# Three pairs of adaLN units through one PSUM bank each, one pair moved onto the second value unit

## The chip, the cores and the metric

The kernel runs on one core of one Trainium2 chip. The metric is the device time of one execution in microseconds, and of several runs the median. The core's engines are TensorE (PE in the profile, with its weight loads as PEld), VectorE (DVE), ScalarE (ACT), GpSimd (POOL) and SyncE (SP), whose queue issues nearly all of the DMAs.

## The reference, cut to what matters

One layer of a streaming encoder is computed for a prompt of 1024 rows and a sample of 32 rows. A conditioning vector for each of the two gives six vectors of 1024 numbers, which scale and shift the rows:

```
mod = jax.nn.silu(c) @ w_ada + b_ada
sh1, sc1, g1, sh2, sc2, g2 = jnp.split(mod[:, None, :], 6, axis=-1)
h = x * (1 + sc1) + sh1
...split(h @ w_in, split_at, axis=-1)        # keys, queries, values of three kinds of heads, gates
mix = jnp.concatenate([mLSTM heads, FoX heads, gated MLP], axis=-1) @ w_o
x = _layer_norm(ALPHA * x + (1 + g1) * mix, ln1_g, ln1_b)
h = x * (1 + sc2) + sh2
y = (jax.nn.silu(h @ w_gate) * (h @ w_up)) @ w_down
x = _layer_norm(ALPHA * x + (1 + g2) * y, ln2_g, ln2_b)
```

`w_ada` has 1024 rows and 6144 columns. `c` is one vector for the prompt and one for the sample, so its product has two rows.

## The kernel before, in words

**adaLN units.** The 6144 columns of `w_ada` are laid out as 24 units of 256 columns. Units 0 to 7 give sh1 and sc1, units 8 to 15 sh2 and sc2, units 16 to 19 g1, units 20 to 23 g2. `ada_load` loads a unit as two tiles of 128x1024 floats (512 KB each), one for each half of the 1024 rows. `ada_parts` then does the unit's work. Eight matmuls of 256 columns (two halves by four quarters of a half; each is two passes in the trace) use a weight tile of 32 columns, `c32`, in which columns 0 and 1 hold the two conditioning vectors and the others are zero. The quarter `k` of a half goes to the PSUM partitions from 32k on, so the two rows of the result stand four times, as partial sums. ACT copies the 128x256 block to `adas`, PE transposes it in two 128x128 pieces into the other half of the same bank (pool `pt`, two banks), and a reduction of DVE into `adam` adds the four partial sums. `ada_end` adds the bias and writes `mod`.

**Where the units stand.** Units 0 to 7 run inside `fm_first`, the first projection. In `run` the list `rest` holds units 16 to 19 and then 8 to 15, and `more(n)` does the next n of them with the tiles `late` (two buffers in pool `pl`). The tuple `T1` says how many come before the first value unit, between the two value units, after the second, and after the first step of the gates: 1, 1, 0, 2. The others come one by one among the heads (`a` in `ORDER`). Units 20 to 23 come near the end of the first half, among the last three key and query units (heads 5, 6, 7): 20 and 21 after head 5, 22 after head 6, 23 after head 7, with six buffers `late`.

**The value units.** `tm_unit` with `w_in_v` computes 264 columns (four heads of values and some gate columns) for nine tiles of rows: first the 32 sample rows (tile 8, 64 small matmuls from the raw weights `tm_raw`), then eight tiles of 128 rows, 24 matmuls each (`tm_g`, pool `pg`, three banks). Weights are split into a high part (ACT, `tm_whi`) and a low part (DVE, `tm_wlo`). `evac_v` copies each bank by ACT into `tm_traw` (two buffers), which the queue of SP stores to `o_v`; DVE makes `tm_vhl` (two buffers) of it, stored to `dv`.

**What sets the order.** `fm_first` is pinned in the order written. The rest is ordered by a scheduler that works on modelled times, so that a step can end up between the steps of another function; `tie` can hold instructions behind a given one. All engines run their instructions in that order. The DMAs of SP's queue are issued in the queue's order, and one that waits for its data or its buffer holds back those behind it.

## Time and profile before

| | |
|---|---|
| median of 3 runs | 1350.47 us (1349.51 to 1352.93) |
| the profiled execution | 1349.43 us, of it 1347.7 us span from the first to the last instruction |
| PE busy | 1326.7 us, 98% of the span |
| DVE, ACT, POOL busy | 992.0, 657.6, 229.2 us |
| mean granted PE clock | 0.997 |
| DMA | 221.73 MB, mean 165 GB/s |

In the profile's timeline a row gives the start in us, the duration, the engine, the line and operation, the tile written and the tiles read, the number of instructions merged into the row, and in brackets the idle time of the engine before it with what ended it. Matmuls are pipelined: the durations of neighbours overlap, so the time that a step takes on PE is read from one start to the next.

### The profile page before, as it was taken

What the parts mean: (1) busy time and instruction counts of PE and PEld (TensorE: products, weight loads), DVE (VectorE), ACT (ScalarE), POOL (GpSimd) and SP (SyncE); (2) the same over time, 40 slices, a digit from 0 to 9 for tenths busy, and PEclk for the clock granted to TensorE, in tenths of its full rate; (3) what the DMA queues carried; (4) which work ended last, traced back from release to release, by engine and by line L of the source; (5) the groups of instructions that cost most, each with busy time, mean ns of one, the idle gap of its engine ahead of it and who ended that gap; (6) DMA issues with size and microseconds to landing.
All of it is one profiled execution on the core that took longest, in us unless ns stands there. A gap on an engine that the chain in (4) does not pass through costs nothing.

```text
span 1347.7 us, 25627 instructions
## 1 busy us (share of the span) xinstructions
PE 1326.7 (98%) x9690; PEld 1209.8 (90%) x9690; DVE 992.0 (74%) x2094; ACT 657.6 (49%) x1308; POOL 229.2 (17%) x263
## 2 busy tenths in 40 slices
PE   9999999999999999999999999999999999999996
PEld 6789888988999888888888888999999999999995
DVE  5635665678779677686876766678988897888777
ACT  3423445454546544545455354436764453635355
POOL 0101100153246100000000000463710000000341
PEclk9999999999999999999999999999999999999998
DMA  9584566545667744454433433673695858554221
GB/s 363 208 288 152 159 193 195 174 118 193 178 225 232 215 123 137 118 146 121 141 107 111 127 87 98 205 186 114 183 266 141 224 152 222 137 177 133 87 79 67
DMA packets 119450, 221.73 MB, mean 165 GB/s; under 512 B 18580, under 2 KB 62768, under 8 KB 119328
## 3 DMA queue, kind: packets, MB, share of 16 engines
q1 hardware_dynamic: 112096, 207.55, 48.9%
q0 software_dynamic: 6032, 11.94, 5.2%
q8 instruction: 76, 1.25, 0.4%
q10 hardware_dynamic: 1200, 0.62, 0.2%
q14 instruction: 46, 0.38, 0.1%
HBM read 188.13 MB, written 51.85 MB: 178 GB/s over the span
## 4 chain that ended last, share of the span: by engine, by line
PE 71%; DVE 3%; ACT 1%; DMA 1%; issue 0%; DVEq 0%; ACTq 0%
PE up_g L129 6%; PE up_g L130 6%; PE up_g L131 6%; PE dn_g L129 4%; PE dn_g L131 4%; PE dn_g L130 4%; PE sup_u L129 3%; PE sup_u L131 3%; PE sup_u L130 3%; PE wo_g L129 2%; PE wo_g L131 2%; PE wo_g L130 2%; PE sup_g L131 2%; PE sup_g L130 2%; PE sup_g L129 2%; PE fox_t L936 2%
## 5 line engine op out<-in xcount | busy, mean ns | idle before, releaser
L130 PE MATMUL up_g<-tm_al,up_whi 128*128 128x512 f32 (+1 forms) x384 | 140.5, 366 | 0.0
L129 PE MATMUL up_g<-tm_ah,up_whi 128*128 128x512 f32 (+1 forms) x384 | 140.1, 365 | 0.0
L131 PE MATMUL up_g<-tm_ah,up_wlo 128*128 128x512 f32 (+1 forms) x384 | 139.4, 363 | 0.0
L1361 ACT CAST sup_whi<-sup_raw 128x1024 fp32r<-128x1024 f32 x54 | 56.0, 1047 | 90.6 <-PE dn_u L130 47.2
L129 PEld LDWEIGHTS up_g<-tm_ah,up_whi 128*128 128x128 f32 x384 | 72.2, 188 | 11.2 <-issue 0.4
L131 PEld LDWEIGHTS up_g<-tm_ah,up_wlo 128*128 128x128 f32 x384 | 72.3, 188 | 11.0
L130 PEld LDWEIGHTS up_g<-tm_al,up_whi 128*128 128x128 f32 x384 | 72.3, 188 | 10.9
L1192 DVE SCALAR_TENSOR_TENSOR wo_z<-dn_g,start_mod,wo_z 128x512 f32<-128x512 f32 (+4 forms) x120 | 60.3, 521 | 26.0 <-PE dn_g L131 25.2
L909 ACT ACTIVATE fox_p<-fox_s,fox_fmx 128x384 f32<-128x384 f32 (+2 forms) x96 | 55.1, 578 | 48.0 <-DVE fox_fmx L907 34.0
L116 ACT CAST up_whi<-up_raw 128x1024 fp32r<-128x1024 f32 x50 | 52.4, 1047 | 51.6 <-PE up_g L130 23.3
L1362 DVE TENSOR_TENSOR sup_wlo<-sup_raw,sup_whi 128x1024 fp32r<-128x1024 f32 x54 | 68.1, 1264 | 10.8 <-ACT sup_whi L1361 10.8
L117 DVE TENSOR_TENSOR up_wlo<-up_raw,up_whi 128x1024 fp32r<-128x1024 f32 x50 | 65.2, 1303 | 13.9 <-ACT up_whi L116 11.6
L131 PE MATMUL dn_g<-up_acth,dn_wlo 128*128 128x512 f32 (+2 forms) x200 | 73.4, 367 | 0.0
L129 PE MATMUL dn_g<-up_acth,dn_whi 128*128 128x512 f32 (+2 forms) x200 | 73.2, 367 | 0.0
L130 PE MATMUL dn_g<-up_actl,dn_whi 128*128 128x512 f32 (+2 forms) x200 | 72.8, 365 | 0.0
L941 ACT CAST fox_pth<-fox_t 128x512 fp32r<-128x512 f32 (+1 forms) x80 | 41.8, 542 | 62.5 <-PE fox_t L936 56.5
L116 ACT CAST dn_whi<-dn_raw 128x1024 fp32r<-128x1024 f32 (+1 forms) x44 | 42.7, 970 | 52.3 <-PE up_g L130 18.9
L904 DVE TENSOR_REDUCE fox_fmx<-fox_s 128x1 f32<-128x384 f32 (+2 forms) x96 | 52.8, 553 | 18.7 <-PE fox_s L901 17.6
L942 DVE TENSOR_TENSOR fox_ptl<-fox_t,fox_pth 128x512 fp32r<-128x512 f32 (+1 forms) x80 | 50.0, 632 | 12.5 <-ACT fox_pth L941 12.1
L397 PE MATMUL tm_g<-tm_whi,start_h1h 128*128 128x256 f32 (+1 forms) x192 | 55.3, 288 | 0.7 <-DVE tm_traw L470 0.7
L397 PE MATMUL tm_g<-tm_whi,start_ah 128*128 128x256 f32 (+1 forms) x192 | 54.8, 286 | 0.5 <-DVE tm_brt L457 0.5
L398 PE MATMUL tm_g<-tm_wlo,start_h1h 128*128 128x256 f32 (+1 forms) x192 | 55.1, 287 | 0.0
(682 smaller groups left out, 4762.7 us busy)
## 6 DMA issues: line engine op xcount, KB each, us to landing
up_raw<-w_gu SPq DMA_DIRECT2D x50, 512.0 KB
ada_late<-w_ada SPq DMA_DIRECT2D x32, 512.0 KB
dn_raw<-w_dn SPq DMA_DIRECT2D x28, 512.0 KB
sup_raw<-w_gu SPq DMA_DIRECT2D x20, 512.0 KB
start_dp<-w_gu SPq DMA_DIRECT2D x19, 512.0 KB
start_dp<-w_gu POOLq DMA_DIRECT2D x19, 512.0 KB, 7.8
wo_raw<-w_o SPq DMA_DIRECT2D x18, 512.0 KB
sup_raw<-start_dp SPq DMA_DIRECT2D x18, 512.0 KB
```

The source lines that it names most:

```text
L116: nc.scalar.copy(hi[:, :w], raw[:, :w])
L117: (eng or nc.vector).tensor_tensor(lo[:, :w], raw[:, :w], f(hi[:, :w]), ALU.subtract)
L129: nc.tensor.matmul(ps, hi, xh(k), start=start and k == 0, stop=False)
L130: nc.tensor.matmul(ps, hi, xl(k), start=False, stop=False)
L131: self.lastmm = nc.tensor.matmul(ps, lo, xh(k), start=False, stop=stop and k == n - 1)
L397: nc.tensor.matmul(ps[:, :ncol], xh, hi, start=k == 0, stop=False)
L398: nc.tensor.matmul(ps[:, :ncol], xh, lo, start=False, stop=False)
L904: nc.vector.tensor_reduce(mxs[:, x:x + 1], s[:, :w], AX.X, ALU.max, negate=True)
L909: nc.scalar.activation(pr[:, lo:hi], banks[x][:, :hi - lo], AF.Exp, bias=mxs[:, 0:1], accum_out=sums[:, x:x + 1])
L1192: self.lastz = self.nc.vector.scalar_tensor_tensor(z[:, m, x:y], ps[:, x - a:y - a], g[i], z[:, m, x:y], ALU.mult, ALU.add)
L1361: nc.scalar.copy(h, x)
L1362: tt(l, x, f(h), ALU.subtract)
```

## The change

`ada_parts` takes a list of units. With two of them it issues all 16 matmuls into one bank: the weights of the second are read from `c32` with an offset, so that its two rows come to stand behind those of the first, and `c32` is 38 columns wide for it, the two vectors in columns 6 and 7. There is then one copy, one pair of transposes and one reduction (into 2 by 8 columns) for both units; `ada_end` runs for each.

Units 16 and 17 form a pair. Its four tiles get a pool of their own, `pe`, with four buffers on the other side of the memory, and it is emitted behind tile 0 of the second value unit, its PE instructions held behind that tile's last matmul. `T1` becomes (0, 0, 0, 2). Units 20 and 21 form a pair after head 6, units 22 and 23 one after head 7; nothing stands after head 5 any more. All other units stay single. The tiles `ct` and `ce`, which are used only at the start, are taken from the weights' buffers in place of the constants' pool.

```diff
-T1 = (1, 1, 0, 2)
+EB = 4
+T1 = (0, 0, 0, 2)
...
-        self.ct = t([P, KT, 2], "ct")
+        self.ct = self.t(self.wp, [P, KT, 2], F32, "whi", WB)
...
-        e = t([P, KT, 2], "ce")
+        e = self.t(self.wp, [P, KT, 2], F32, "wlo", WB)
...
-    def ada_parts(self, u, raws, ppool, ptag):
+    def ada_parts(self, units, raws, ppool, ptag):
         self.phase = "ada"
         nc = self.nc
+        n = len(units)
         ps = self.t(ppool, [P, 512], F32, ptag)
-        for i, half in enumerate((0, 1) if ptag == "t" and u < 8 else (1, 0)):
+        steps = [(i, half) for half in ((0, 1) if units[0] < 8 else (1, 0)) for i in range(n)[::1 if half else -1]]
+        for step in steps:
+            i, half = step
             for k in range(4):
-                nc.tensor.matmul(ps[32 * k:32 * k + 32, :256], self.c32[:, 4 * half + k, :],
-                                 raws[half][:, k * 256:(k + 1) * 256], start=i == 0, stop=i == 1)
+                nc.tensor.matmul(ps[32 * k:32 * k + 32, :256], self.c32[:, 4 * half + k, 6 - 2 * i:38 - 2 * i],
+                                 raws[i][half][:, k * 256:(k + 1) * 256], start=step == steps[0],
+                                 stop=step == steps[-1])
...
-        m = self.t(self.pada, [P, 4], F32, "adam", 2)
-        nc.vector.tensor_reduce(m.rearrange("p (h j) -> p h j", h=2), pt.rearrange(
-            "p (h g j) -> p h j g", h=2, g=4)[:, :, 0:2, :], AX.X, ALU.add)
-        self.ada_end(u, m)
+        m = self.t(self.pada, [P, 2, 8], F32, "adam", 2)[:, :, :2 * n]
+        nc.vector.tensor_reduce(m, pt.rearrange("p (h g j) -> p h j g", h=2, g=4)[:, :, 0:2 * n, :], AX.X, ALU.add)
+        for i, u in enumerate(units):
+            self.ada_end(u, m[:, :, 2 * i:2 * i + 2])
...
-        self.c32 = self.t(self.cst, [P, KT, 32], F32, "c32")
+        self.c32 = self.t(self.cst, [P, KT, 38], F32, "c32")
         nc.vector.memset(self.c32, 0.0)
-        nc.vector.tensor_copy(self.c32[:, :, 0:2], self.cs)
+        nc.vector.tensor_copy(self.c32[:, :, 6:8], self.cs)
...
-        rest = list(range(16, 20)) + list(range(8, 16))
+        rest = [18, 19] + list(range(8, 16))
...
         more(T1[0])
+        se = ExitStack()
+        pe = self.pool("pe", ctx=se, side="right")
+
+        def group(units):
+            def go():
+                first = len(nc.cur_bb.bb.instructions)
+                target = self.lastmm
+                for _ in self.ada_parts(units, raws, self.pt, "t"):
+                    pass
+                self.tie(nc.cur_bb.bb.instructions[first:], target, (mybir.EngineType.PE,))
+                self.phase = "tm"
+            raws = [self.ada_load(u, pe, "early", EB) for u in units]
+            return go
+
         self.tm_unit(w1[0], 264, self.evac_v(0))
-        more(T1[1])
-        self.tm_unit(w1[1], 264, self.evac_v(1))
+        self.tm_unit(w1[1], 264, self.evac_v(1), between={0: group((16, 17))})
+        se.close()
...
-                for u in (20, 21) if u == 0 else (21 + u,):
-                    self.ada(u, pq, "late", 6, self.pt, "t")
+                if u:
+                    self.ada((18 + 2 * u, 19 + 2 * u), pq, "late", 6, self.pt, "t")
```

What the scheduler makes of it is seen in the instructions' order. On PE between the two value units stood, before, the matmuls of unit 17 and its transposes, in the midst of the sample tile's small matmuls (`tm_raw`); unit 16 stood inside tile 4 of the first value unit:

```order
L399 MATMUL tm_g_980<-tm_whi_704,start_h1l_172 128x264
L198 MATMUL ada_t_1017<-ada_late_1015,start_c_62_182 32x256 x4
L198 MATMUL ada_t_1017<-ada_late_1013,start_c_62_182 32x256 x4
L409 MATMUL tm_g_1047<-tm_raw_1041,start_hs_173 32x66 x16
L409 MATMUL tm_g_1047<-tm_raw_1035,start_hs_173 32x66 x15
L206 MATMUL ada_t_1017<-start_ident_120,ada_adas_1026 128x128 x2
L409 MATMUL tm_g_1047<-tm_raw_1035,start_hs_173 32x66
L397 MATMUL tm_g_1088<-tm_whi_1037,start_ah_169 128x264
```

The same place now, and after it the end of tile 0 (`tm_g_1055`) and of tile 1 (`tm_g_1117`):

```order
L404 MATMUL tm_g_961<-tm_whi_685,start_h1l_172 128x264
L416 MATMUL tm_g_1014<-tm_raw_1008,start_hs_173 32x66 x16
L416 MATMUL tm_g_1014<-tm_raw_1002,start_hs_173 32x66 x16
L402 MATMUL tm_g_1055<-tm_whi_1004,start_ah_169 128x264
...
L404 MATMUL tm_g_1055<-tm_whi_1010,start_al_170 128x264
L202 MATMUL ada_t_1088<-tm_early_996,start_c_62_182 32x256 x4
L202 MATMUL ada_t_1088<-tm_early_1000,start_c_62_182 32x256 x4
L202 MATMUL ada_t_1088<-tm_early_998,start_c_62_182 32x256 x4
L202 MATMUL ada_t_1088<-tm_early_994,start_c_62_182 32x256 x4
...
L211 MATMUL ada_t_1088<-start_ident_120,ada_adas_1105 128x128 x2
```

Nothing of adaLN stands between the value units any more; the pair's matmuls follow tile 0, and its transposes come 23 matmuls later.

On the queue of SP, from the store of tile 1 of the first value unit on, stood before (`ada_late_674` and `676` are unit 16, `1013` and `1015` unit 17; `o_v` and `start_dv` are a tile's two stores):

```order
L86 DMA ada_late_674<-w_ada 128x1024
L86 DMA ada_late_676<-w_ada 128x1024
L90 DMA o_v<-tm_traw_840 128x256
L86 DMA gates_mo_1355<-state_m 4x1
L90 DMA start_dv_59<-tm_vhl_844 128x512
L90 DMA o_v<-tm_traw_873 128x256
L90 DMA start_dv_59<-tm_vhl_877 128x512
L90 DMA o_v<-tm_traw_906 128x256
L90 DMA start_dv_59<-tm_vhl_910 128x512
L86 DMA head_v_1477<-start_dv_59 128x4x128
L86 DMA ada_late_1013<-w_ada 128x1024
L86 DMA ada_late_1015<-w_ada 128x1024
```

and now (`tm_early` are units 16 and 17, `ada_late_1420` and `1422` unit 18):

```order
L87 DMA tm_early_994<-w_ada 128x1024
L87 DMA tm_early_996<-w_ada 128x1024
L91 DMA o_v<-tm_traw_821 128x256
L87 DMA tm_early_998<-w_ada 128x1024
L87 DMA tm_early_1000<-w_ada 128x1024
L91 DMA start_dv_59<-tm_vhl_825 128x512
L87 DMA ada_late_1420<-w_ada 128x1024
L87 DMA ada_late_1422<-w_ada 128x1024
L91 DMA o_v<-tm_traw_854 128x256
L91 DMA start_dv_59<-tm_vhl_858 128x512
L91 DMA o_v<-tm_traw_887 128x256
L91 DMA start_dv_59<-tm_vhl_891 128x512
```

Four loads of 512 KB, of units 17 and 18, have moved ahead of the stores of tile 3 (`tm_traw_873` before, `854` now), and the two loads `head_v` have moved behind the stores of the second value unit's first tile.

On PE among the late key and query units stood before, in head 7's first product (`fm_g_5795`), the matmuls of unit 21 with the transposes of unit 20 between the first and the second of them:

```order
L131 MATMUL fm_g_5795<-start_h1h_171,fm_wlo_5792 128x272
L198 MATMUL ada_t_5674<-ada_late_5672,start_c_62_182 32x256
L206 MATMUL ada_t_5652<-start_ident_120,ada_adas_5661 128x128 x2
L198 MATMUL ada_t_5674<-ada_late_5672,start_c_62_182 32x256 x3
L198 MATMUL ada_t_5674<-ada_late_5670,start_c_62_182 32x256 x4
L129 MATMUL fm_g_5795<-start_h1h_171,fm_whi_5791 128x272
```

and now the pair 20 and 21 at the end of head 6, its transposes in head 7, and the pair 22 and 23 behind head 7 (`ada_late_5836` and `5838` are unit 23):

```order
L202 MATMUL ada_t_5728<-ada_late_5722,start_c_62_182 32x256 x4
L202 MATMUL ada_t_5728<-ada_late_5726,start_c_62_182 32x256 x4
L202 MATMUL ada_t_5728<-ada_late_5724,start_c_62_182 32x256 x4
L202 MATMUL ada_t_5728<-ada_late_5720,start_c_62_182 32x256 x4
...
L211 MATMUL ada_t_5728<-start_ident_120,ada_adas_5745 128x128 x2
...
L202 MATMUL ada_t_5840<-ada_late_5834,start_c_62_182 32x256 x4
L202 MATMUL ada_t_5840<-ada_late_5838,start_c_62_182 32x256 x4
L202 MATMUL ada_t_5840<-ada_late_5836,start_c_62_182 32x256 x4
L202 MATMUL ada_t_5840<-ada_late_5832,start_c_62_182 32x256 x4
```

The matmuls of a pair now stand together, with no transposes between them. From the end of tile 1 of the second value unit to head 6 PE's order is the one of before. Behind this place, among the first feed-forward products and the heads woven into them, some neighbouring instructions have changed places on PE, DVE and ACT; the order on POOL is the same.

More of the change, by code (lines that the diff above doesn't have):

```diff
@@ L177, in constants, with ada @@
         self.sf = t([72, NS], "sf")
[L180 removed]
+    def ada(self, units, pool, tag, bufs, ppool, ptag):
         self.phase = "ada"
[L182 removed]
+        for _ in self.ada_parts(units, [self.ada_load(u, pool, tag, bufs) for u in units], ppool, ptag):
             pass
@@ L382, in fm_first, with tm_unit @@
             self.store(self.dmqk[:, m], out[m])
-    def tm_unit(self, src, ncol, evac, tiles=range(9), eng=None):
+    def tm_unit(self, src, ncol, evac, tiles=range(9), eng=None, between={}):
         nc = self.nc
@@ L398, in tm_unit @@
                 nc.tensor.matmul(ps[:, :ncol], xh, lo, start=False, stop=False)
-                nc.tensor.matmul(ps[:, :ncol], xl, hi, start=False, stop=k == 7)
+                self.lastmm = nc.tensor.matmul(ps[:, :ncol], xl, hi, start=False, stop=k == 7)
             evac(tt, ps, P)
+            if tt in between:
+                between[tt]()
     def sample_tile(self, w, ncol, evac):
```

8 lines of the change are left out of this document (3 added, 5 removed).

## The prediction

> **What bounds the kernel now.** I read the page's busy times first, then who waited for whom on PE, then PE's timeline where adaLN units stand, and last the timelines of ACT and SP's queue and the DMA's share at these places.
>
> ```profile
> span 1347.7 us, 25627 instructions
> PE 1326.7 (98%) x9690; PEld 1209.8 (90%) x9690; DVE 992.0 (74%) x2094; ACT 657.6 (49%) x1308; POOL 229.2 (17%) x263
> ```
>
> PE is busy for all but 21 us, so the time falls by what is taken from PE's own work and from its waits, and by nothing else. Its waits at adaLN units, with the total, the number and the longest:
>
> ```profile
> PE ada_t L198 <- DMA ada_late<-w_ada: 1.6, 1, 1.6
> PE ada_t L206 <- ACT ada_adas L201: 1.3, 2, 0.8
> ```
>
> These two are among the longest waits of PE in the whole program. Everything that the change can win is in PE's path around the units it moves, a few microseconds of 1348; a measurement of this kernel can tell a difference from none at about 0.3%, here 4.05 us.
>
> **Part 1: what one unit costs on PE.** Unit 16 ran in the midst of tile 4 of the first value unit, where nothing waits. First its matmuls, then its transposes, with the neighbouring products:
>
> ```profile
> 75.99 0.28 PE L398 MATMUL tm_g<-tm_wlo,start_h1h 128*128 128x264 f32 x1
> 76.21 1.07 PE L198 MATMUL ada_t<-ada_late,start_c 128*32 128x256 f32 x16
> 77.21 0.39 PE L399 MATMUL tm_g<-tm_whi,start_h1l 128*128 128x264 f32 x1
> 77.44 0.28 PE L397 MATMUL tm_g<-tm_whi,start_h1h 128*128 128x264 f32 x1
> 77.56 0.28 PE L398 MATMUL tm_g<-tm_wlo,start_h1h 128*128 128x264 f32 x1
> ...
> 79.97 0.29 PE L397 MATMUL tm_g<-tm_whi,start_h1h 128*128 128x264 f32 x1
> 80.09 0.38 PE L206 MATMUL ada_t<-start_ident,ada_adas 128*128 128x128 f32 x2
> 80.23 0.37 PE L398 MATMUL tm_g<-tm_wlo,start_h1h 128*128 128x264 f32 x1
> 80.43 0.29 PE L399 MATMUL tm_g<-tm_whi,start_h1l 128*128 128x264 f32 x1
> ```
>
> A product's step is 77.56 - 77.44 = 0.12. From 75.99 to 77.44 two product steps were done, so the 16 passes and the way in and out cost 1.45 - 0.24 = 1.21. The passes themselves are 77.21 - 76.21 = 1.00 of it, and 0.21 is the detour. The two transposes cost 80.43 - 79.97 - 0.24 = 0.22. A unit is 1.43. A pair has 32 passes, one detour and one pair of transposes: 2.00 + 0.21 + 0.22 = 2.43. Against two units, 2.86, each pair saves 0.43, the three 1.29. The trace has no run of 32 passes; if they filled better or worse than twice 16 it would show within the 0.21 on either side.
>
> ```profile
> L206 PE MATMUL ada_t<-start_ident,ada_adas x48: 270/272/328, 8.1 to 447.5; 128*128 128x128 f32 x48
> ```
>
> The duration of one transpose is 0.27, but in the pipeline two of them move the next product by only 0.22, and I take the latter. The Trainium skill ("TensorE: Matmul & The Clock Gate", Part 4: PE-mode transpose) gives about 275 ns for one in a kernel's context; as a duration the trace agrees (272 ns), and if six of them cost that much in PE's path, the sum below would be larger by 1.63 - 0.66 = 0.97.
>
> **Part 2: the pair 16 and 17.** Unit 17 stood between the value units. Below are the last product of the first value unit (84.47), the start of unit 17, its transposes and the first product of tile 0 (89.74); above them, for comparison, the sample tile of the first value unit (L409) and its first product:
>
> ```profile
> 58.64 1.13 PE L409 MATMUL tm_g<-tm_raw,start_hs 128*32 128x66 f32 x64
> 59.70 0.39 PE L397 MATMUL tm_g<-tm_whi,start_ah 128*128 128x264 f32 x1
> ...
> 84.47 0.28 PE L399 MATMUL tm_g<-tm_whi,start_h1l 128*128 128x264 f32 x1
> 86.40 1.07 PE L198 MATMUL ada_t<-ada_late,start_c 128*32 128x256 f32 x16 [1.64 <-DMA ada_late<-w_ada]
> 89.14 0.44 PE L206 MATMUL ada_t<-start_ident,ada_adas 128*128 128x128 f32 x2 [0.76 <-ACT ada_adas L201]
> ...
> 89.74 0.39 PE L397 MATMUL tm_g<-tm_whi,start_ah 128*128 128x264 f32 x1
> ```
>
> The sample tile of the first value unit, undisturbed, takes 59.70 - 58.64 = 1.06 to the next product; with 0.22 to get from a product into it (as from 75.99 to 76.21) the way from 84.47 to 89.74 would be 1.28. It is 5.27, so unit 17 costs 3.99: its work of 1.43, and 2.56 of waiting, of which the rows name 1.64 for its load and 0.76 for ACT's copy, which is late since ACT first did others. The change takes out 1.43 + 3.99 = 5.42 here and puts in 2.43 behind tile 0: a gain of 2.99. The load's wait goes because the four tiles no longer wait for unit 16's buffers; the copy's wait goes because 23 products (23 x 0.12 = 2.8) now stand between the matmuls and the transposes, in the place of 31 small ones.
>
> What could be late next is the bank of tile 5, which the sample tile takes over, three banks being in turn. ACT must have copied it, into one of two `tm_traw`, whose store of tile 3 must have landed. SP's queue and ACT's copies of tiles 2, 4 and 5 in before:
>
> ```profile
> 68.22 1.74 SPq L86 DMA_DIRECT2D ada_late<-w_ada  x2
> 71.04 0.34 SPq L90 DMA_DIRECT2D o_v<-tm_traw  x1
> 78.45 0.98 SPq L86 DMA_DIRECT2D ada_late<-w_ada  x2
> ...
> 70.64 0.38 ACT L427 COPY tm_traw<-tm_g 128x264 f32<-128x264 f32 x1 [4.42 <-DMA o_v<-tm_traw]
> 76.18 0.38 ACT L427 COPY tm_traw<-tm_g 128x264 f32<-128x264 f32 x1 [4.10 <-DMA o_v<-tm_traw]
> 78.75 0.38 ACT L427 COPY tm_traw<-tm_g 128x264 f32<-128x264 f32 x1 [1.04 <-PE tm_g L399]
> ```
>
> The copies at 70.64 and 76.18 waited for a store: that of tile 2, issued at 71.04 behind unit 16's 1 MB, had landed at 76.18, after 5.1. The store of tile 3 follows it by a position or two and had landed before 78.75, when the copy of tile 5 waited for PE alone; I put its landing at 77 to 77.9. In the order of now four loads of 512 KB, 2.1 MB, stand ahead of this store. What the DMA moved in stretches, the last two numbers being its share and GB/s:
>
> ```profile
> 72.00:74.00 2.00, 2.00 (x18) 2.00 (x18) 0.79 (x3) 0.08 (x1) 0.00 (x0) 1.00 1.01 390
> 74.00:76.00 2.00, 2.00 (x19) 2.00 (x17) 0.00 (x0) 0.00 (x0) 0.00 (x0) 1.00 0.84 312
> ...
> 80.00:82.00 2.00, 2.00 (x19) 2.00 (x18) 0.70 (x4) 0.10 (x1) 0.00 (x0) 1.00 1.06 196
> ```
>
> At 390 GB/s the 2.1 MB take 5.4 and the store lands at 82.4 to 83.3; at 312 they take 6.7, and it lands at 83.7 to 84.6. The copy takes 0.38. The sample tile would want the bank at 84.47 - 1.43 + 0.22 = 83.26. So the new wait is between nothing and 84.6 + 0.38 - 83.26 = 1.7. I take nothing, since these are weight loads in large pieces as in the stretch at 390, and keep 1.7 for the range. The low weights of k from 4 on are the next: ACT's cast of them stands behind tile 5's copy, 1.1, then DVE's subtraction, 1.3, so 82.8 + 2.4 = 85.2 against a need at 83.26 + 1.06 + 12 x 0.12 = 85.8: covered, and 0 to 1 late when the copy is.
>
> **Part 3: the pairs 20 and 21, 22 and 23.** Units 20 and 21 in before:
>
> ```profile
> 433.00 0.29 PE L131 MATMUL fm_g<-start_h1h,fm_wlo 128*128 128x272 f32 x1
> 433.21 0.62 PE L198 MATMUL ada_t<-ada_late,start_c 128*32 128x256 f32 x2
> 433.76 0.44 PE L206 MATMUL ada_t<-start_ident,ada_adas 128*128 128x128 f32 x2
> 434.13 1.06 PE L198 MATMUL ada_t<-ada_late,start_c 128*32 128x256 f32 x14
> 435.12 0.40 PE L129 MATMUL fm_g<-start_h1h,fm_whi 128*128 128x272 f32 x1
> 435.36 0.29 PE L130 MATMUL fm_g<-start_h1l,fm_whi 128*128 128x272 f32 x1
> ```
>
> From 433.00 to 435.36, less two product steps, 2.12 went by for one unit's matmuls and one unit's transposes, 1.43 by part 1. The other 0.69 was lost where the transposes stood between the first and second matmul. The four units cost 4 x 1.43 + 0.69 = 6.41, the two pairs 2 x 2.43 = 4.86: a gain of 1.55.
>
> What could be late next are the tiles of unit 23. Six buffers hold three units, and the last two loads need buffers of the first pair:
>
> ```profile
> 430.95 1.89 SPq L86 DMA_DIRECT2D ada_late<-w_ada  x2
> ...
> 443.04 1.07 PE L198 MATMUL ada_t<-ada_late,start_c 128*32 128x256 f32 x16
> ```
>
> In before they were issued at 430.95 and wanted at 443.04, 12 later. Now they need the end of the pair's 32 passes, about 431.5 in before's time, and the store between them in SP's order, so the second goes out at about 433; the second pair stands 48 products and two transposes behind, at 437.7, and wants that tile 0.5 later. This leaves some 5 us for 512 KB, and the store above took 5.1 behind 1 MB. The wait is between nothing and the 7.95 that unit 17's load took (issued at 78.45, landed at 86.40) less 5, that is 2.9. I take nothing, since the two loads stand alone here, and keep 2.9.
>
> **Part 4: edits taken at nothing.** Three copies fewer on ACT and three reductions fewer on DVE are off PE's path (49% and 74% busy). The columns added to `c32` make one memset of DVE at the start a fifth longer; DVE waits for POOL's masks behind it, and without that cover the first unit would start later by this fifth. `ct` and `ce` take a turn in the weights' buffers long before those are reused; without that cover PE's start would be late by one load. The loads `head_v` moved behind stores are for heads that run after the gates. The swaps among the first feed-forward products lie where PE hardly waits; they can win next to nothing, and I keep 0.5 to lose.
>
> **The sum.** 2.99 + 1.55 = 4.54 (pairs 1.29, waits 2.56, interleaving 0.69). From the profiled execution, 1349.43 (span 1347.7, 1.7 around it), this gives 1344.9; that execution is 1.0 below the median, so against the median it is 1350.47 - 4.5 = 1346.0.
>
> **The rivals.** A: as summed, no new wait over half a microsecond.
>
> B: the gain comes, and part goes back into the two new waits of parts 2 and 3, 1 to 3 us in all: 1347 to 1349. For it: the margins are below 1 us at both places. Against: at both the row nearest leaves it covered.
>
> C: the stores of the first value unit come so late behind the loads that PE loses more than it wins. The price: if the queue drains at the slowest full stretch (196 GB/s, 80 to 82, when the loads `head_v` stood in it), the 2.1 MB take 10.7, the store of tile 3 lands at 87.7 to 88.6, and PE waits 4.8 to 5.7 at the sample tile and about 0.8 at tile 0, since the cast stands between the copies; with part 3's 2.9 it is 8.5 to 9.4 at the most. Less 4.5 that is 1.1 to 4.9 above before, 1351.6 to 1355.4. It decides from the point where the store lands after 87.4 (83.26 + 4.5 - 0.38). Against it: `head_v`, in small pieces, no longer runs there. The Trainium skill ("DMA: Bandwidth & Descriptors", Queues, rings and completion order) has each DMA engine take descriptors in ring order, so that a store stands behind every load issued before it; by that rule, the trace agrees, as the store of 71.04 landed 5.1 later.
>
> The idle time that ended at 86.4 has another name on PEld, with the instruction it names:
>
> ```profile
> 86.37 0.62 PEld L198 LDWEIGHTS ada_t<-ada_late,start_c 128*32 128x32 f32 x16 [1.82 <-DVE tm_wlo L117]
> ...
> 84.44 1.26 DVE L117 TENSOR_TENSOR tm_wlo<-tm_raw,tm_whi 128x1056 fp32r<-128x1056 f32 x1 [1.29 <-ACT tm_whi L116]
> ```
>
> D: the change does not take the wait away, since it was not the load's. If the sample tile waits there for something else, DVE's work for one, 1.64 stays: 1347.6. Against: that subtraction ended at 85.7, 0.7 before PE went on.
>
> **How the numbers follow.** A 0.56, B 0.25, C 0.14, D 0.05. The bound of 0.3% is at 1346.4, close to A's 1346.0: of A 0.48 is faster and 0.08 the same; of B 0.02 and 0.23; D is the same; of C 0.06 is the same and 0.08 slower. Faster 0.50, same 0.42, slower 0.08. The range goes from A with transposes at their full duration and half a microsecond of the runs' scatter (1346.0 - 0.97 - 0.5 = 1344.5) to B's end with the same run scatter of up to 1.5 (1350.5); most of C is left out.
>
> **What would show it.** Right: no PE row between the value units names a load or `ada_adas`; the sample tile of the second value unit starts near 83.3 and tile 0 near 84.3; the pair's passes start behind tile 0 and take about 2.0; behind the tiles of the value unit all of PE's rows are 3.0 earlier, behind the first pair of up products 4.5. Wrong, and B or C: PE waiting for `tm_traw` of ACT at the sample tile or tile 0, or for the DMA of `ada_late` at the second late pair.

## The result, and the profile after

| | before | after |
|---|---|---|
| median of 8 runs each, side by side | 1348.99 us (1348.14 to 1352.93) | 1345.22 us (1344.11 to 1348.22) |
| the profiled execution, and its span | 1349.43, 1347.7 us | 1346.69, 1344.9 us |

The ratio is 0.9972, 95% interval 0.9962 to 0.9981: 3.8 us faster, 0.28%, just under the 0.3% that the prediction called the limit of what can be told, with the limit inside the interval. In two later sittings, with 11 and 7 runs, the same kernel stood at 0.9964 (0.9954 to 0.9974) and 0.9976 (0.9966 to 0.9987), 4.9 and 3.6 us by the medians. The forecast was 4.5 us, to 1346.0.

The page's span and busy time of PE after:

```profile
span 1344.9 us, 25607 instructions
PE 1324.0 (98%) x9684; PEld 1208.3 (90%) x9684; DVE 989.1 (74%) x2091; ACT 655.8 (49%) x1305; POOL 231.9 (17%) x263
```

PE's own work fell by 2.7 us. Who waited for whom on PE, with total, number and longest, the larger rows that differ from before:

```profile
PE fox_o L951 <- DVE fox_ptl L949: 1.1, 1, 1.1
...
PE up_u L132 <- DVE up_wlo L118: 0.8, 1, 0.8
PE dn_g L130 <- DVE wo_z L1199: 0.8, 1, 0.8
PE tm_g L416 <- ACT tm_traw L434: 0.7, 1, 0.7
...
PE ada_t L211 <- ACT ada_adas L206: 0.6, 1, 0.6
```

The load of `ada_late` (1.6) is gone and so is the later one of the two waits for `ada_adas`; the 0.6 that is left is unit 0's at the program's start. In their place stands 0.7 for a copy of a value tile, the new wait that the prediction named and put at nothing. The three waits for DVE lie far behind the change.

PE's timeline after, at the second value unit (the last product of the first unit, the sample tile, the first product of tile 0, then the pair and the products around it):

```profile
82.69 0.29 PE L404 MATMUL tm_g<-tm_whi,start_h1l 128*128 128x264 f32 x1
83.64 1.13 PE L416 MATMUL tm_g<-tm_raw,start_hs 128*32 128x66 f32 x64 [0.66 <-ACT tm_traw L434]
84.89 0.39 PE L402 MATMUL tm_g<-tm_whi,start_ah 128*128 128x264 f32 x1
...
87.80 0.28 PE L404 MATMUL tm_g<-tm_whi,start_al 128*128 128x264 f32 x1
88.01 1.93 PE L202 MATMUL ada_t<-tm_early,start_c 128*32 128x256 f32 x32
89.88 0.39 PE L402 MATMUL tm_g<-tm_whi,start_ah 128*128 128x264 f32 x1
90.11 0.29 PE L403 MATMUL tm_g<-tm_wlo,start_ah 128*128 128x264 f32 x1
```

From 82.69 to 84.89 are 2.20 where 1.28 would be undisturbed, 0.92 more: the 0.66 that the row names, and the rest before tile 0. The pair takes 90.11 - 87.80 - 0.24 = 2.07. What PE waited for is on ACT's timeline after, the copies of tiles 4, 5 and 6:

```profile
76.46 0.38 ACT L434 COPY tm_traw<-tm_g 128x264 f32<-128x264 f32 x1 [4.68 <-DMA o_v<-tm_traw]
83.20 0.38 ACT L434 COPY tm_traw<-tm_g 128x264 f32<-128x264 f32 x1 [6.37 <-DMA o_v<-tm_traw]
...
84.46 0.38 ACT L434 COPY tm_traw<-tm_g 128x264 f32<-128x264 f32 x1
```

ACT stood idle 6.37 us until the store of tile 3 had landed at 83.2, and PE with it at the end. Tile 0 takes over the bank of tile 6, whose copy ended at 84.84, 0.05 before tile 0 began. The late pairs on PE after:

```profile
427.00 0.29 PE L132 MATMUL fm_g<-start_h1h,fm_wlo 128*128 128x272 f32 x1
427.22 1.93 PE L202 MATMUL ada_t<-ada_late,start_c 128*32 128x256 f32 x32
429.08 0.39 PE L130 MATMUL fm_g<-start_h1h,fm_whi 128*128 128x272 f32 x1
...
435.56 2.17 PE L202 MATMUL ada_t<-ada_late,start_c 128*32 128x256 f32 x32
437.67 0.38 PE L130 MATMUL up_g<-tm_ah,up_whi 128*128 128x256 f32 x1
```

Nothing stands between the matmuls of two units any more. The second pair is 0.24 longer than the first (2.17 against 1.93). In a third profile of this kernel (the run e8_after_third below) it is 0.39 longer, and there the row names the cause, the load of unit 23:

```profile
435.70 0.64 PE L202 MATMUL ada_t<-ada_late,start_c 128*32 128x256 f32 x8
436.52 1.50 PE L202 MATMUL ada_t<-ada_late,start_c 128*32 128x256 f32 x24 [0.18 <-DMA ada_late<-w_ada]
```

In the first profile PE's own row names nothing, but the weight loads of the same matmuls (PEld) stood idle 0.52 us for this DMA. So the second wait that the prediction put at nothing came too, as a few tenths.

To see where time was won or lost I subtracted the starts of the same matmuls in two traces, the median over 8 us behind each point (points in us of the kernel before's profile; negative is earlier than there):

| us | 60 | 110 | 230 | 260 | 350 | 425 | 460 | 940 | 1020 | 1335 |
|---|---|---|---|---|---|---|---|---|---|---|
| after, 1st profile | -0.35 | -2.60 | -2.63 | -1.43 | -2.61 | -2.55 | -4.27 | -4.63 | -2.37 | -2.49 |
| after, 2nd | -0.36 | -1.50 | -1.53 | -0.75 | -2.10 | -1.64 | -3.44 | -3.81 | -3.63 | -3.75 |
| after, 3rd | -0.07 | -2.57 | -2.60 | -2.27 | -2.56 | -2.40 | -3.98 | -4.35 | -4.19 | -4.31 |

The value units are left behind at 110, the late units between 425 and 460. The second and third profile are those of the runs e3_after_again and e8_after_third below. Three executions of one program agree on the late units (1.72, 1.80, 1.58), differ at the value units (2.25, 1.14, 2.50) and in between: at 230 to 260, where PE may wait for `fox_ptl`, and at 940 to 1020, where the first profile lost 2.3 us and the others 0.2.

### The profile page after: what moved, and what is told of

Its sections match the earlier page's. It is cut to its first block, busy times and chain, and to the rows that moved or that the text cites. A ratio compares the mean times of both kernels' runs of the same rounds, so it can differ in the third digit from the quotient of the medians.

```text
span 1344.9 us, 25607 instructions
## 1 busy us (share of the span) xinstructions
PE 1324.0 (98%) x9684; PEld 1208.3 (90%) x9684; DVE 989.1 (74%) x2091; ACT 655.8 (49%) x1305; POOL 231.9 (17%) x263
## 4 chain that ended last, share of the span: by engine, by line
PE 68%; DVE 4%; DMA 1%; ACT 1%; issue 1%; DVEq 0%; ACTq 0%
PE up_g L130 6%; PE up_g L132 6%; PE up_g L131 6%; PE dn_g L130 4%; PE dn_g L132 4%; PE dn_g L131 4%; PE sup_u L132 3%; PE sup_u L131 3%; PE sup_u L130 3%; PE wo_g L131 2%; PE wo_g L132 2%; PE wo_g L130 2%; PE sup_g L132 2%; PE sup_g L131 2%; PE sup_g L130 2%; PE fox_t L943 2%
## 5 line engine op out<-in xcount | busy, mean ns | idle before, releaser
L118 DVE TENSOR_TENSOR dn_wlo<-dn_raw,dn_whi 128x1024 fp32r<-128x1024 f32 (+1 forms) x44 | 49.5, 1125 | 10.4 <-ACT dn_whi L117 9.5
L1320 POOL DMA_DIRECT2D start_dp<-w_gu x19 | 19.8, 1067 | 209.0 <-DMA start_dp<-w_gu 209.0
```

The source lines that it names most:

```text
L118: (eng or nc.vector).tensor_tensor(lo[:, :w], raw[:, :w], f(hi[:, :w]), ALU.subtract)
```

## The experiments

All have the same two questions behind them: which place gives how much, and what the new wait is made of. The theory to start with (1) was that the gains of the two places add and pass on to the end; its rival (2) that the waits for DVE at 970 to 1013 take part of them back in a regular way.

**The early pair alone, and the late pairs alone.** Of the changed kernel, the first takes units 20 to 23 back to where they were, each by itself; the second takes back units 16 and 17.

```diff
-                if u:
-                    self.ada((18 + 2 * u, 19 + 2 * u), pq, "late", 6, self.pt, "t")
+                for v in (20, 21) if u == 0 else (21 + u,):
+                    self.ada((v,), pq, "late", 6, self.pt, "t")
```

> Only units 16 and 17 are a pair behind tile 0 of the second value unit; units 20 to 23 are single, as before. Theory 1 (the gain is the sum of what is taken from PE at the places of the units, and the rest of the program passes it on): behind the value units PE is 2.3 to 3.0 earlier than before (2.99 less the wait for tile 5's bank, 0.66 in the changed kernel's profile), nothing is gained at the late units, and the median is 2.3 to 3.0 below before. Theory 2 (DVE, or a chain over DMAs, sets the pace at later places and takes gains back, as at 970 to 1013 us of the changed kernel's profile): PE is 2.3 to 3.0 earlier at 130 us, but the median is less than 1.5 below before, and the profile shows the same waits for DVE at 970 to 1013.

```diff
-T1 = (0, 0, 0, 2)
+T1 = (1, 1, 0, 2)
...
-        rest = [18, 19] + list(range(8, 16))
+        rest = list(range(16, 20)) + list(range(8, 16))
...
-        self.tm_unit(w1[1], 264, self.evac_v(1), between={0: group((16, 17))})
+        more(T1[1])
+        self.tm_unit(w1[1], 264, self.evac_v(1))
```

> Only the pairs 20 with 21 and 22 with 23 are made; units 16 and 17 are single and stand where they stood before. Theory 1: PE runs as before up to the late units, is 1.3 to 1.6 earlier behind them (two pairs at 0.43 and 0.69 of interleaving), and the median is 1.3 to 1.6 below before. Theory 2: 1.3 to 1.6 earlier at 460 us, and the median within 0.7 of before.

**The changed kernel again, and its places without sharing.** The second keeps all units where the change put them, but each has a bank, a copy and transposes of its own.

> The changed kernel once more, for a second profile. Theory 1: the waits for DVE and for fox_ptl at 237 and at 970 to 1013 us (3.3 us in all in the first profile) differ from execution to execution: they are absent or of another size here, and PE is 4.0 to 4.7 earlier than before from 460 to 910 us again. Theory 2: the same waits stand at the same places with the same sizes, 2 us in all at 970 to 1013.

```diff
-                for _ in self.ada_parts(units, raws, self.pt, "t"):
-                    pass
+                parts = [self.ada_parts((u,), (raws[i],), self.pt, "t") for i, u in enumerate(units)]
+                weave(*parts)
...
-                    self.ada((18 + 2 * u, 19 + 2 * u), pq, "late", 6, self.pt, "t")
+                    for v in (18 + 2 * u, 19 + 2 * u):
+                        self.ada((v,), pq, "late", 6, self.pt, "t")
```

> The units stand where the change puts them, with the loads it gives them, but every unit has its own bank, copy, transposes and reduction: nothing is shared. Theory 1: 0.43 is lost to the changed kernel at units 16 and 17, and 0.86 and the interleaving of up to 0.69 at units 20 to 23, so the median is 1.3 to 2.0 above the changed kernel and 2 to 2.7 below before. Rival (the sharing is worth nothing, since the pair's work is only pushed together and the waits are all there was): within 0.3 of the changed kernel at 130 us.

Measured beside one another, before at 1349.93 us:

| | median us | ratio | gain at 60 to 110 | at 425 to 460 |
|---|---|---|---|---|
| early pair alone | 1347.19 | 0.9981 (0.9972 to 0.9989) | 2.15 | 0.22 |
| late pairs alone | 1348.21 | 0.9986 (0.9976 to 0.9995) | -1.11 | 1.72 |
| the changed kernel | 1345.06 | 0.9964 (0.9954 to 0.9974) | 1.14 | 1.80 |
| its places, no sharing | 1346.32 | 0.9970 (0.9958 to 0.9982) | 2.48 | 0.41 |

2.74 and 1.72 make 4.5, and both together gave 4.9. Theory 2 falls: in the second profile the loss at 970 to 1013 isn't there, though PE was 3.4 to 3.8 earlier from 460 to 940 and not the 4.0 to 4.7 expected, since it had waited longer at the value units. Sharing by itself is 1.3 us of it (1346.32 against 1345.06; the prediction had 1.29), though the intervals of these two overlap; the kernel without sharing stood 3.6 below before, not the 2 to 2.7 expected. At the value units it gained 2.48, as much as the changed kernel, which looks as if sharing were worth nothing there. But by the rows it lost only 0.43 at the bank where the changed kernel lost more (next section); with this added back it stands at 2.91 against 3.15 to 3.17, so sharing is worth about 0.25 there. That is one pair of transposes and not the whole 0.43 of part 1: the 32 passes of its two units also ran in one piece. Without sharing the late units gained only 0.41, and one reason is seen on PE's timeline of that kernel: the scheduler put one unit's transposes between another's matmuls again:

```profile
430.70 1.06 PE L202 MATMUL ada_t<-ada_late,start_c 128*32 128x256 f32 x14
431.70 0.44 PE L211 MATMUL ada_t<-start_ident,ada_adas 128*128 128x128 f32 x2
432.07 0.62 PE L202 MATMUL ada_t<-ada_late,start_c 128*32 128x256 f32 x2
```

The kernel with the late pairs alone shows something else. Its unit 17 waits for the load as in before, but a little longer. PE's timeline, then the stretches behind it (busy time of PE, PEld, DVE, ACT and POOL, the granted PE clock, the DMA's share and GB/s):

```profile
86.54 1.55 PE L202 MATMUL ada_t<-ada_late,start_c 128*32 128x256 f32 x16 [2.05 <-DMA ada_late<-w_ada]
87.79 2.05 PE L416 MATMUL tm_g<-tm_raw,start_hs 128*32 128x66 f32 x62
```

```profile
87.00:88.00 1.00, 1.00 (x20) 0.69 (x15) 0.00 (x0) 0.32 (x2) 0.00 (x0) 0.50 0.51 193
88.00:89.00 1.00, 1.00 (x48) 1.00 (x43) 0.44 (x2) 1.00 (x3) 0.00 (x0) 0.50 0.13 49
```

After 2.05 us of idleness the clock is at 0.50, the 16 passes take 1.55 in place of 1.07, the sample tile 2.05 in place of 1.12. The kernel before had waited 1.64 at this place with the clock at 1.00 behind it.

**The new wait: a third buffer, and unit 18's loads later.** The second profile of the changed kernel waited longer at the bank than the first:

```profile
PE tm_g L416 <- ACT tm_traw L434: 1.3, 1, 1.3
...
PE tm_g L402 <- ACT tm_traw L434: 0.6, 1, 0.6
```

So the rows that name this wait have 0.4 (third profile) to 1.9 us. Read from the last product of the first value unit to the first of tile 0, less the 1.28 of the prediction, its price in the three profiles is 0.92, 2.03 and 0.65. Two edits should take it away in different ways.

```diff
-            raw = self.t(self.sm, [P, 264], F32, "traw", 2)
+            raw = self.t(self.pe, [P, 264], F32, "vraw", 3)
...
-        pe = self.pool("pe", ctx=se, side="right")
+        pe = self.pe = self.pool("pe", ctx=se, side="right")
```

> The changed kernel with three buffers instead of two for ACT's copy of a value tile (the second value unit's too). Theory 'two buffers': at the sample tile of the second value unit PE waited 0.66 us (first profile of the changed kernel), 1.9 us with tile 0 (its second profile), because ACT's copy of tile 5 needs the buffer of tile 3, whose small store is queued behind the loads; with a third buffer PE's wait for ACT tm_traw is gone at the sample tile and at tile 0, PE is 3.2 to 4.4 us earlier than in the kernel before at 110 us (changed kernel: 2.6 and 1.5), and the time is 0.7 to 1.9 us below the changed kernel's. Rival 'the queue': the copy of tile 5 would have been late for another reason, or the pair's loads, which stand later in SP's row here, are waited for instead: the same 1.5 to 2.6 us at 110 us, and no gain.

```diff
-            self.load(raws[half], self.d["w_ada"][u, :, half * 1024:(half + 1) * 1024])
+            x = self.load(raws[half], self.d["w_ada"][u, :, half * 1024:(half + 1) * 1024])
+            if u == 18:
+                self.tc.add_manual_dep(x.ins, self.st5.ins.name, mybir.DependencyInfo(
...
+            st = self.store(self.d["o_v"][tt * P:(tt + 1) * P, cols], raw)
+            if half == 0 and tt == 5:
+                self.st5 = st
```

> The changed kernel with unit 18's two loads (512 KB each) put behind the stores of tiles 3, 4 and 5 of the first value unit in SP's row; nothing else differs. If the wait at the sample tile is the store of tile 3 behind the loads: 1.05 MB less ahead of it, it lands some 2.7 us earlier, PE waits under 0.2 us for ACT tm_traw, is 3.0 to 4.4 us earlier than in the kernel before at 110 us, and the time is 0.7 to 1.9 us below the changed kernel's; unit 18's own matmuls, after the first step of the gates, are not late. If not: wait and time within 0.5 us of the changed kernel's.

> The changed kernel once more beside the three others. By the sum of what the places gave (2.7 from the early pair, 1.7 from the late ones) 4.4 us below the kernel before. If waits later on take it back in a regular way, as the first profile of the changed kernel had it between 970 and 1013 us: 2 to 2.5 us below.

Measured beside one another (before 1349.70): the changed kernel 1346.12, 0.9976 (0.9966 to 0.9987); three buffers 1344.50, 0.9964 (0.9951 to 0.9978); unit 18 later 1345.00, 0.9968 (0.9956 to 0.9981). In both profiles the wait at the sample tile is gone. PE's timeline at the sample tile with three buffers:

```profile
83.60 1.13 PE L416 MATMUL tm_g<-tm_raw,start_hs 128*32 128x66 f32 x64
```

and ACT's copy of tile 5 with unit 18 later (this execution stands 1.18 later than the first of the changed kernel already at 60):

```profile
81.53 0.38 ACT L437 COPY tm_traw<-tm_g 128x264 f32<-128x264 f32 x1 [3.71 <-DMA o_v<-tm_traw]
```

The copy that started at 83.20 + 1.18 = 84.38 by the changed kernel's pace started at 81.53, 2.85 earlier with 1.05 MB less in the queue; the expectation was 2.7, from 390 GB/s. Set against the second and third profile in the same way it is 3.5 and 2.6 earlier. From 60 to 110 this kernel gained 3.18, against 2.25, 1.14 and 2.50 in the three profiles of the changed kernel. Adding back to these the 0.92, 2.03 and 0.65 gives 3.17, 3.17 and 3.15, and the same sum for the early pair alone, 2.15 and 1.00, gives 3.15. So the wait explains all that was missing at the value units.

At 110 PE was 2.84 and 2.35 earlier than before, where 3.2 to 4.4 and 3.0 to 4.4 were expected. With unit 18 later that is the late start of this execution. With three buffers PE gained 3.15 from 74 to 110, but it had lost 0.54 at 68, where it waited for a copy of another value tile (a row of 0.28). The gains in time, 1.6 and 1.1 us, are of the size expected, but the intervals overlap.

**A dose.** Two and then four loads of 512 KB that nothing reads, ahead of the late stores.

```diff
             raws = [self.ada_load(u, pe, "early", EB) for u in units]
+            self.ada_load(19, pe, "extra", 2)
```

> The changed kernel with two more loads of 512 KB (unit 19's, read by nothing) in SP's row ahead of the store of tile 3 of the first value unit: a dose of what rival C of the prediction is made of. If that store lands after the loads queued ahead of it: 1.05 MB at about 390 GB/s are 2.7 us, so PE's wait at the sample tile of the second value unit goes from 0.66 to 1.9 us (two profiles of the changed kernel) to 3.3 to 4.6 us, and the time is 2.0 to 3.0 us above the changed kernel's. If the store does not queue behind the loads, the wait stays under 2 us and the time within 0.7 us.

```diff
+            for u in (18, 19):
+                self.ada_load(u, pe, "extra", 4)
```

> The changed kernel with four more loads of 512 KB (read by nothing) ahead of the late stores of the first value unit: twice the dose, 2.1 MB, at 390 GB/s 5.4 us. With two such loads PE waited 1.5 us before tile 0 and then ran 16 products at a granted clock of 0.5, which cost as much again. Theory 'length and clock': the waits between the last product of the first value unit and tile 0 come to 4 to 5.5 us, the clock falls to 0.5 behind them in the profile, and the time is 4.5 to 7.5 us above the changed kernel's, so 0 to 3 us above the kernel before. Theory 'length alone' (the low clock was an accident of that run): 3 to 4.5 us above the changed kernel's, and the clock 1.0.

The first gave 1347.26, 0.9985 (0.9974 to 0.9995), 1.1 above the changed kernel, and its sample tile waited no longer (0.54 us): this expectation was missed. On SP the scheduler had put unit 18's loads behind the store of tile 3 in exchange, so the same 3 MB stood ahead of it, and the dose ahead of tile 4's store. Tile 6's copy came late for it, and tile 0 got its bank only after the sample tile's copy. PE with two more loads, then the stretches:

```profile
83.52 1.13 PE L416 MATMUL tm_g<-tm_raw,start_hs 128*32 128x66 f32 x64 [0.54 <-ACT tm_traw L434]
86.19 0.39 PE L402 MATMUL tm_g<-tm_whi,start_ah 128*128 128x264 f32 x1 [1.54 <-ACT tm_tmsum L420]
```

```profile
84.00:86.00 2.00, 0.65 (x47) 0.48 (x36) 1.52 (x3) 1.97 (x6) 0.00 (x0) 1.00 0.93 356
86.00:88.00 2.00, 1.81 (x9) 1.81 (x10) 1.97 (x7) 0.90 (x3) 0.00 (x0) 0.63 0.76 154
88.00:90.00 2.00, 2.00 (x11) 2.00 (x11) 0.79 (x6) 0.00 (x0) 0.00 (x0) 0.52 1.07 354
```

The waits are 1.42 longer than the changed kernel's, and its products ran at half the clock until 90: from the first product of tile 0 to the pair 4.66 in place of 3.12, another 1.5. With four more loads the waits and the clock behind them were:

```profile
84.80 1.13 PE L416 MATMUL tm_g<-tm_raw,start_hs 128*32 128x66 f32 x64 [1.62 <-ACT tm_traw L434]
87.47 0.59 PE L402 MATMUL tm_g<-tm_whi,start_ah 128*128 128x264 f32 x1 [1.54 <-ACT tm_tmsum L420]
```

```profile
88.00:90.00 2.00, 2.00 (x11) 2.00 (x10) 0.94 (x4) 0.00 (x0) 0.00 (x0) 0.50 1.04 399
90.00:92.00 2.00, 2.00 (x11) 2.00 (x10) 0.86 (x3) 0.71 (x2) 0.00 (x0) 0.50 1.05 423
```

Waits of 3.16 in all, below the 4 to 5.5 expected, and then the low clock again: the gain at the value units of the first profile turned into 4.95 less, about half of it by waits (3.16 - 0.66) and half by the clock. The time, 1349.79, 0.9994 (0.9983 to 1.0005), is 0.4 below before. Against the changed kernel, which stood in the sitting before, it is 3.7 more by the medians and 2.4 by the two ratios, under the range of "length and clock" (4.5 to 7.5), and by the medians inside that of "length alone" (3 to 4.5). The profile speaks for length and clock. The other executions have no profile, but a mean clock each: a stretch of 3.4 us at half the clock takes, by an estimate (3.41 x 0.5 of 1349), 0.0013 off it. Eight of the eleven runs stand at 0.994 to 0.996, with a median of 1350.1 us, and three at 0.997, with one of 1346.5; of the changed kernel's 26 runs 5 stand below 0.997. So in most executions, not in all, the loads seem to have cost a stretch of low clock, and in the three others next to nothing.

**Three buffers without the change.** The control for the third buffer, with its repetition beside it:

```diff
+        se = ExitStack()
+        self.pe = self.pool("pe", ctx=se, side="right")
         self.tm_unit(w1[0], 264, self.evac_v(0))
...
-            raw = self.t(self.sm, [P, 264], F32, "traw", 2)
+            raw = self.t(self.pe, [P, 264], F32, "vraw", 3)
```

(The new pool is closed behind the second value unit.)

> The kernel before with three buffers instead of two for ACT's copy of a value tile, and nothing of the change. If the third buffer gives back only what the change itself made PE wait for (0.4 to 1.9 us at the sample tile): PE did not wait for ACT tm_traw in the kernel before, whose load wait at the sample tile (1.64 us) is untouched, so its time stays within 0.7 us of the kernel before. If the buffer is worth something of its own: 1 to 2 us below it.

> The changed kernel with three buffers for the copies of the value tiles, once more, beside the same buffers without the change. If its gain over the changed kernel (1344.5 against 1346.1 us) is real: 5 to 6 us below the kernel before, no PE wait for the copies at the sample tile. If it was scatter: 3.8 to 4.9 us below, as the changed kernel's.

Both expectations for the control were missed: 1345.28, 0.9971 (0.9959 to 0.9982), 4.9 below before (1350.17) by the medians and 3.9 by the ratio, without any pair. The changed kernel with three buffers stood at 1345.33, 0.9965 (0.9951 to 0.9979), next to it. That is 4.8 below before, in the range named for scatter (3.8 to 4.9) and not in that of a real gain (5 to 6): what the third buffer adds to the change isn't confirmed. On PE the control's unit 17 no longer waits for its load:

```profile
84.21 1.07 PE L198 MATMUL ada_t<-ada_late,start_c 128*32 128x256 f32 x16
```

On SP's queue (SPq) it stands with its issue at 77.02, in before at 78.45 behind a load `head_v`:

```profile
77.02 0.86 SPq L86 DMA_DIRECT2D ada_late<-w_ada  x2
```

With three buffers the scheduler moved `head_v` behind it, as the change had done. So the wait that the pair removed (2.5 us of this kernel's gain lie between 60 and 110) can be removed with unit 17 in its old place too. A last kernel asked what the early pair adds to that: three buffers and the late pairs.

> Three buffers for the copies of the value tiles and the two late pairs, units 16 and 17 each by itself as in the kernel before: the early pair is the only thing that it lacks of the changed kernel with three buffers. Three buffers without the change gave 4.9 us, at the value units 2.5 of it by the profile, and the late pairs gave 1.7. If the early pair is worth little once the load of unit 17 is in time (its 0.43 us of a shared unit): 5 to 6.5 us below the kernel before, no PE wait for ada_late at the sample tile of the second value unit. If the early pair is still worth its 2.7 us: 2 to 3.5 us below the kernel before.

This kernel stood at 1345.57, 0.9971 (0.9958 to 0.9983), 4.4 below before, between the two expectations. In its profile the load was late again:

```profile
85.82 1.07 PE L202 MATMUL ada_t<-ada_late,start_c 128*32 128x256 f32 x16 [1.32 <-DMA ada_late<-w_ada]
```

In its queue too no `head_v` stands ahead of unit 17's loads; they were issued at 77.87, behind a store at 77.44. So a third buffer alone leaves unit 17's load on the edge, 0 us late in one profile and 1.3 in another, and the place of `head_v` doesn't decide it alone; the early pair takes it off that edge. By the ratios the kernel with three buffers on top of the change is the lowest in both of its sittings (0.9964 and 0.9965), but the changed kernel itself reached 0.9964 once, so no version is shown to beat it. Nor is it shown to beat the control, which makes no pair at all (0.9971 against 0.9964 to 0.9976).

## Why the prediction came out as it did

- **Part 1, the cost of a pair.** 2.43 was forecast; the early one took 2.07 for passes and detour, and by the rows around its transposes (92.66 to 93.13, less two steps of 0.12) 0.23 for these: 2.30. Passes in a run of 32 are a little cheaper than twice 16, within the 0.21 that was kept. The transposes cost their effect in the pipeline, not their duration: the sum by the Trainium skill's 275 ns ("TensorE: Matmul & The Clock Gate", Part 4: PE-mode transpose) would, as an estimate, have counted 0.55 here, and the 0.23 decides.
- **Part 2, the value units.** Both waits went, as forecast, and nothing else took their place but the bank. What was mis-sized is "I take nothing" for the bank's wait, with up to 1.7 kept. It was 0.92, 2.03 and 0.65. The landing was forecast for 82.4 to 83.3 and was 83.2; what the choice of nothing overlooked is that by its own numbers the copy then ends up to 0.4 after the need, that PE can come earlier (0.35 in the first profile), and that scatter in the queue counts in full. Without this wait the gain was 3.15 to 3.18; the forecast of 2.99 with the pair at 2.30 in place of 2.43 is 3.12. The cause given for the load's wait, unit 16's buffers, was only part of it: in before these were free at 77.28 and the loads were issued at 78.45, behind stores and a `head_v`. In the control, with the same two buffers, they were issued at 77.02 and PE didn't wait for them; with the late pairs added they were issued at 77.87 and PE waited again. Which of the things ahead of them decides stays open.
- **Part 3, the late units.** 1.55 forecast, 1.72, 1.80 and 1.58 measured. The first pair's passes are 0.14 cheaper than forecast. The second's are 0.24, 0.13 and 0.39 longer than the first's, and the third profile names the load of unit 23 for it: the wait put at nothing, with 2.9 kept, was a few tenths.
- **Part 4** was right at the places named, but the prediction didn't say that waits far behind would differ from one execution to the next by as much as its terms. In the first profile of after PE waited 1.1 for `fox_ptl`, in the third 0.2; and before's profile, from which the sum was counted, has a wait that the first two of after lack:

```profile
PE mlstm_s L755 <- DMA mlstm_mv<-start_dmv: 1.2, 1, 1.2
```

- **The sum**, 4.54, came out as 3.8, 4.9 and 3.6 us in three sittings, and the time as 1345.2 where 1346.0 was forecast. That the time was met this closely is in part luck. The median of before was 1.5 lower over the eight runs beside the change than over the three from which the forecast was counted; from 1348.99, A would have been 1344.4 and B 1345.5 to 1347.5. By what happens on PE the three profiles are B's: the bank and the load of unit 23 together took 1.16, 2.16 and 1.04 us, where A allowed half a microsecond and B 1 to 3, and pairs cheaper than forecast gave a part of it back. C's mechanism exists (2.6 to 3.5 us per 1.05 MB in the queue) but wasn't reached. D fell: the wait went with the load.

## What to carry to other kernels

Taking an instruction block out of a place where it waits wins its work and its wait; the place where the next wait stands is then worth a row-by-row sum of its own, and if that sum ends within a microsecond of zero it should be entered at its middle, not at nothing. Before a block is moved because of a late load, look at what stands ahead of this load on its queue: here a third buffer for a store, with the reordering that it brought, removed the same wait in one profile, though not in that of a kernel close to it, and gave a time that isn't told apart from the change's. When two gains of a few microseconds are to be told apart, subtract the starts of the same instructions in two traces and compare the steps at each place, since the end times mix in waits that come and go.

## What was unexpected of the hardware

**Short waits can halve PE's clock.** A wait of 2.05 us (late pairs alone) and one of 1.54 us behind the small matmuls of a sample tile (two more loads) were each followed by 3.4 us at a granted clock of 0.50, so that they cost nearly twice their length; one of 1.64 us in before's profile and two of 1.3 and 0.6 us in the second of after were not. Wherever it fell before the last microseconds of the program, the sample tile's small matmuls or a unit's passes, both of 32 columns, lay beside the wait.

The traces tell more. In four profiles the clock fell before that end, and in each of them it fell a whole number of times 3.41 us after the first entry of its record (24 times 3.41 in three of them, 94 in the fourth; the entry lies between 4.4 and 7.1 us into the span, not at a fixed place), and stayed low for 3.41 us or twice that. So one can lay stretches of 3.41 us on each trace from that entry on, and see how long PE was busy in a stretch and whether the clock fell behind it. Some of them:

| profile | stretch, us | PE busy of 3.41 us | clock behind it |
|---|---|---|---|
| four more loads | 83.11 to 86.52 | 1.19 | 0.50 |
| late pairs alone | 83.58 to 86.99 | 1.36 | 0.50 |
| two more loads | 83.10 to 86.51 | 1.44 | 0.50 |
| three buffers, second profile | 322.23 to 325.64 | 1.74 | 0.50 |
| two more loads, near the end | 1332.37 to 1335.78 | 1.44 | 1.00 |
| after, first profile | 321.1 to 324.5 | 1.70 | 1.00 |
| before | 85.67 to 89.08 | 1.98 | 1.00 |
| three buffers and late pairs | 84.10 to 87.51 | 2.09 | 1.00 |
| after, second profile | 83.61 to 87.03 | 2.17 | 1.00 |

Of all stretches at the full clock inside the spans of the 14 profiles, each with 1.36 us or less of busy PE was followed by the low clock, and none with more than 1.74; between these both happened. What counts is thus the idle time that falls into one such stretch, about half of it, more than the length of one wait: in before the end of a stretch at 85.67 cut the wait of 1.64 us in two. Where between the two numbers the edge lies, and whether matmuls of 32 columns count less, no run here shows. The Trainium skill ("TensorE: Matmul & The Clock Gate", Part 1: The HAM clock gate) has the clock fall after an idle window of about 3.4 us, and the window free-running. The length of the window and that it runs free agree with the traces; that the window is idle doesn't, since PE was busy in up to half of it, so there the measurement decides. Such falls also fit most of the times of whole runs: of the 75 runs of the kernel before beside which the experiments ran, the 10 with a mean clock of 0.995 have a median of 1352.6 us, the 44 with 0.997 one of 1349.7. With three buffers and the late pairs it doesn't: three runs at 0.995 have a median of 1345.6, the others one of 1345.8.

**One program, two profiles.** The changed kernel with three buffers was profiled twice, spans 1341.4 and 1345.3 us. In the second PE waited before the products of a head at 238, and the clock fell at 325, behind a sample tile between waits of 1.0 and 0.7 us, which every profile has, the first of them as 0.6 to 1.1; its row of waits and the stretch:

```profile
PE fox_s L907 <- ACT fox_p L916: 1.7, 1, 1.7
```

```profile
325.00:330.00 5.00, 4.76 (x27) 4.79 (x28) 4.77 (x9) 3.17 (x10) 3.52 (x5) 0.66 0.90 240
```

A difference of 3.9 us between two profiles of one program is as large as the whole change; without repeated profiles the waits of one execution pass for effects of an edit.
